# Gate/up stages of a two-sequence encoder layer: working buffers in neighbouring pairs, and 1024 columns per instruction where there were 512

## The chip, the cores and the metric

The kernel runs on one core of one Trainium2 chip. The metric is the device time of one execution in microseconds (us). Engines are named as the profile names them: PE is the matrix engine, PEld its weight load, DVE the vector engine, ACT the scalar engine, POOL the third general engine, and SPq the queue that issues nearly all DMA transfers. Each engine works through its own list of instructions in the order written for it, and an instruction that waits holds up everything behind it on that engine. A product sum is formed in a bank of PSUM, the memory that PE writes.

## The reference, cut to what matters

One encoder layer is applied to two sequences of 512 tokens, x_prompt and x_sample, with 1024 channels each, in float32. The layer is a half-weighted feed-forward part, a mixing part (attention beside an mLSTM memory, merged by gates), and a second half-weighted feed-forward part; a last norm follows. The feed-forward part is what the change touches:

```
def swiglu(x, w_gate, w_up, w_down):
    return (jax.nn.silu(x @ w_gate) * (x @ w_up)) @ w_down
x = x + 0.5 * swiglu(rms_norm(x, ffn1_norm), ffn1_w_gate, ffn1_w_up, ffn1_w_down)
...
x = x + 0.5 * swiglu(rms_norm(x, ffn2_norm), ffn2_w_gate, ffn2_w_up, ffn2_w_down)
```

w_gate and w_up are 1024 x 2816, w_down is 2816 x 1024. The width 2816 makes 22 blocks of 128 columns.

## The kernel before, in words

Float32 accuracy is got from a narrower matrix format (fp32r): a value is split into a part `hi`, made by a copy on ACT, and the remainder `lo = value - hi`, made by a subtraction on DVE. A product of two split matrices takes three matrix multiplications: hi with hi, hi with lo, lo with hi. So whatever goes into PE, weights and inputs, first costs one ACT and one DVE instruction of its size.

The gate and up products of a block, for both sequences together, form a two by two block product. The kernel does it with seven half-size products in place of eight (a scheme of Strassen's kind). For this it needs sums of weights and sums of inputs. The names are B11, B21, B22, T1, T2_, T3, T4, each a product of a weight half (4 slices of 128 rows) with an input tile `xc[...]` (512 columns wide, both hi and lo). One product is 4 slices times 3 matrix multiplications, that is 12 of 128 x 512.

A gate/up stage (there are two, one for each feed-forward part) runs thus:

- **Start.** `norm_x` and `turn` (stage one) or `turn_rows` (stage two) bring the inputs into place; `right_sums` forms the four sums of inputs per slice and `put` splits them into `xc`. While DVE and ACT do this, PE runs `begin(j)` for the first 7 blocks: products B11 and B21 only. Their two results, called v1 and g0, are parked in DRAM (`kept`). The first sequence's slices are parked in DRAM too (`xnbuf`) and loaded back for the sums.
- **Rest.** `rest` walks over the 22 blocks in the order `ORDER`: a block with kept results (5 products to do: T2_, T1, T3, B22, T4) alternates with a fresh block (7 products: B11, T2_, B21, T1, T3, B22, T4), seven times, and eight fresh blocks follow. Two blocks following each other make a pair here. The weights of the next block are made by `gu_left_a` (B11, B21), `gu_left_b` (T2_, T1, T3, B22) and `gu_left_c` (T4).
- **Out.** `gu_rest` adds the products up (bank Y takes T2_, T3, T4 one after the other, bank Z takes T1, B22) and forms gate times up: two results of 128 x 512 for a block. `Sides.even` and `Sides.odd` turn the four results of a pair into seven split matrices, the right sides of the down product, and write each hi and lo to DRAM (`rbuf`).

The stage that follows, `ffn_down`, reads `rbuf` and does the down product.

Buffers are rings. In `Rings`, `v` has 3 rows of 512 columns, `h` 5, `s` 3, `o` 7 and `wd` 2; rows are handed out one after the other, whatever becomes of the one before. Block number i (from 0) uses h rows 2i and 2i+1 (modulo 5) for g0 and the running sum u2 (lines 304, 305), and both rows stay in use as the in-place source of later sums and outputs: line 346 turns the even block's first result into the value of T1, line 338 writes its lo part over it, and the row is free once that DMA has landed.

Line 307 is the first reader of bank Y in a block: it forms u2 from v1 and the T2_ product, and only then may T3 be added in that bank. Between T2_ and T3 PE has the one product T1 to do in a block with kept results. A scheduler gives each engine its order: program order shifted by `SOONER` (sums that free a bank) or `LATER` (the `Sides` work), and then by its own model of when each instruction can run. Line numbers in the profile are those of the listing here.

In the mixing part the same pool of rows is used through `T2()`: 11 single rows under the tag "t2" and 4 under "f2", besides 2 rows "R" and a table tile whose first three rows serve the gate/up stages.

Of the kernel before, what the change touches and what calls it, by code (L numbers as in the profile page):

```python
# [16 lines left out]
P = 128  # L17
# [9 lines left out]
def encoder(ctx, tc, I, outs):  # L27
# [32 lines left out]
    def T2(dtype=F32, tag="t2"):  # L60
        if tag in ("eb", "ac"):
            i = boxes[tag]
            boxes[tag] += 1
            return boxes["tile"][:, i % 4 + (4 if tag == "ac" else 0), :]
        if tag == "R":
            return spool.tile([P, S], dtype, tag="R", bufs=2, name=nm("R"))
        n = {"t2": 11, "f2": 4}[tag]
        return tpool.tile([P, S], dtype, tag=tag, bufs=n, name=nm(tag))
# [14 lines left out]
    class Rings:  # L83


        def __init__(self, **kinds):
            self.rows = {k: [T2(F32, t) for t in tags] for k, tags in kinds.items()}
            self.at = dict.fromkeys(kinds, 0)

        def join(self, kind, *of):  # L90

            self.rows[kind] = [t for k in of for t in self.rows[k]]
            self.at[kind] = 0

        def rest(self, kind):

            rows = self.rows[kind]
            i = self.at[kind] % len(rows)
            return rows[i:] + rows[:i]

        def __call__(self, kind, dtype=F32):
            rows = self.rows[kind]
            t = rows[self.at[kind] % len(rows)]
            self.at[kind] += 1
            return t if dtype is F32 else t.bitcast(dtype)
# [124 lines left out]
    def right_sums(xc, k, x0l, x0u, x1l, x1u):  # L230
# [5 lines left out]
        for i, t in ((T1, x0l), (T2_, x1u), (T3, x1l), (T4, x0u)):  # L236
            put(xc[i], k, t)
# [17 lines left out]
    def gu_left_b(rg, ru, ring):  # L255
        v = lambda t: t.rearrange("p (k c) -> p k c", c=P)
        a, b = v(ring("s")), v(ring("s"))
        wb, wc = w8_tile(), w8_tile()
        V_.tensor_tensor(a, half(ru, 0), half(ru, 1), op=ALU.add)
        w_pair(wb[:, :, 1], a)  # L260
        V_.tensor_tensor(b, half(rg, 0), half(ru, 0), op=ALU.subtract)
        V_.tensor_tensor(a, a, half(rg, 0), op=ALU.subtract)  # L262
        w_pair(wb[:, :, 0], a)
        w_pair(wc[:, :, 0], b)
        V_.tensor_tensor(a, half(rg, 1), a, op=ALU.subtract)
        w_pair(wc[:, :, 1], a)
        return {T2_: part(wb, 0), T1: part(wb, 1), T3: part(wc, 0), B22: part(wc, 1)}

    def gu_left_c(ru, ring):
        wd = [ring("wd", F32R).rearrange("p (k c) -> p k c", c=P) for _ in range(2)]  # L270
        split(half(ru, 1), *wd)
        return {T4: wd}
# [23 lines left out]
    def gu_rest(W, xc, got, ring, mid):  # L296

        Y, Z = PS(), PT()
        second = lambda: product(Y, W[T2_], xc[T2_], True)
        if got:  # L300
            v1, g0 = got
            second()
        else:
            v1, g0 = gu_first(W, xc, lambda i: ring("vh"[i]), second)
        u2 = ring("h")
# [3 lines left out]
        v5 = ring("v")  # L309
# [16 lines left out]
        V_.tensor_tensor(g0, g0, v1, op=ALU.mult)  # L326
        V_.tensor_tensor(u2, u2, v5, op=ALU.mult)
        return g0, u2

    class Sides:  # L330


        def __init__(self, rb, ring):
            self.rb, self.ring = rb, ring

        def out(self, i, src, last=False):
            hi = self.ring("o")
            lo = src if last else self.ring("o")
            nc.scalar.activation(hi.bitcast(F32R), src, AF.Copy)
            V_.tensor_tensor(lo.bitcast(F32R), src, hi, op=ALU.subtract)  # L340
            nc.sync.dma_start(self.rb[i][:, 0, :], hi)
            nc.sync.dma_start(self.rb[i][:, 1, :], lo)

        def even(self, b11, b12):
            self.out(B11, b11)
            V_.tensor_tensor(b11, b12, b11, op=ALU.subtract)
            self.b = b11, b12

        def odd(self, b21, b22):
            t1, b12 = self.b  # L350
            self.out(B21, b21)
            self.out(B22, b22)
            V_.tensor_tensor(b12, b22, b12, op=ALU.subtract)
            self.out(T3, b12, True)
            V_.tensor_tensor(b22, b22, t1, op=ALU.subtract)
            self.out(T1, t1, True)
            V_.tensor_tensor(b21, b21, b22, op=ALU.subtract)
            self.out(T2_, b22, True)
            self.out(T4, b21, True)
# [6 lines left out]
    class Up:  # L366


        def __init__(self, xc, wg, wu, rb):
# [3 lines left out]
            self.ring = Rings(s=["t2"] * 3, wd=["f2"] * 2, v=["t2"] * 3, h=["t2"] * 5, o=["f2"] * 2 + ["R"] * 2)  # L373
            self.ring.rows["o"] += tables(FFN_ROWS)
            self.ring.join("x", "v", "h")
            self.ring.rows["k"], self.ring.at["k"] = self.ring.rows["o"][:2], 0
# [4 lines left out]
        def begin(self, j, W):  # L381

            self.kept[j] = kept[j]
            for t, d in zip(gu_first(W, self.xc, lambda _: self.ring("k")), kept[j]):
# [5 lines left out]
        def rest(self, raw, at=None, hook=None):  # L390
            ring = self.ring

            def resume(j):
                got = ring("v"), ring("h")
                for t, d in zip(got, self.kept.pop(j)):
                    nc.sync.dma_start(t, d)
                return got

            left = gu_left_b(*raw, ring)
            left.update(gu_left_c(raw[1], ring))  # L400
            raw = self.fetch(ORDER[1])
            got = resume(ORDER[0])
            for i, j in enumerate(ORDER):
                W = left
                nxt = ORDER[i + 1] if i + 1 < NF else None
                if nxt is not None:
                    left = {} if nxt in self.kept else gu_left_a(raw[0])
                    left.update(gu_left_b(*raw, ring))
                    ru = raw[1]
# [4 lines left out]
                if nxt is not None:  # L414
# [999 lines left out]
```

## Time and profile before

| what | value |
|---|---|
| median of 3 runs | 2124.43 us (2123.21 to 2124.66) |
| the profiled execution | 2124.45 us, its span 2122.7 us |
| busy | PE 98%, PEld 80%, DVE 74%, ACT 46%, POOL 5% |
| granted clock of PE, mean | 0.994 |
| gate/up stage one, first product to the down product | 20.42 to 458.14 us |
| gate/up stage two, the same | 1466.44 to 1898.43 us |
| DMA, mean over the span | 170 GB/s |

The profile counts time from the first instruction. A line of a group gives line number, engine, operation, output and input, size and count, then busy time, mean duration in ns, and idle time before with what ended it. The chain of waits follows the work back from the last instruction. The timeline lists instructions in order of time with start and duration, equal ones merged; a number in brackets is idle time before them and what ended it. Matrix multiplications overlap, so that a merged row's duration is somewhat longer than the distance from its start to the next.

### The profile page before, as it was taken

How to read it: one execution, taken by the hardware profiler on the slowest of the kernel's cores; microseconds unless marked ns; L12 is line 12 of the kernel's file. 1: busy time of each engine (PE TensorE's matmuls, PEld its weight loads, DVE VectorE, ACT ScalarE, POOL GpSimd, SP SyncE). 2: the span in 40 equal slices, each digit the busy share in tenths (PEclk: the TensorE clock that was granted, in tenths of full speed). 3: DMA queues.
4: the chain of work that ended last, by engine and by line, in shares of the span. 5: the costliest groups of instructions: out<-in, count | busy, mean ns of one | idle time of the engine just before them, and what ended most of it. 6: DMA issues, size and time to landing. Idle time of an engine off the chain costs nothing.

```text
span 2122.7 us, 26809 instructions
## 1 busy us (share of the span) xinstructions
PE 2070.4 (98%) x9472; PEld 1687.7 (80%) x9472; DVE 1581.2 (74%) x2817; ACT 968.5 (46%) x1739; POOL 107.2 (5%) x110
## 2 busy tenths in 40 slices
PE   6999999999999999999999999999999999999997
PEld 5887788888888777878887787788777888888885
DVE  7888787776796796574668855764988887786696
ACT  6544444442225466464435654544644444443223
POOL 0000000001000110100102001010000000000002
PEclk9999999999999999999999999999999999999998
DMA  8455554389764212232342122354454554479753
GB/s 272 150 195 194 182 188 144 133 300 395 270 230 158 74 66 68 92 114 88 120 158 80 60 90 74 135 171 157 164 194 163 199 172 159 144 262 389 287 205 121
DMA packets 141270, 361.81 MB, mean 170 GB/s; under 512 B 15600, under 2 KB 15616, under 8 KB 140112
## 3 DMA queue, kind: packets, MB, share of 16 engines
q1 hardware_dynamic: 140544, 358.84, 48.0%
q0 software_dynamic: 592, 1.27, 0.3%
q8 instruction: 74, 1.21, 0.2%
q14 instruction: 60, 0.49, 0.1%
HBM read 255.15 MB, written 104.89 MB: 170 GB/s over the span
## 4 chain that ended last, share of the span: by engine, by line
PE 81%; DVE 10%; ACT 4%; DMA 4%; issue 2%; POOL 0%; SPq 0%; ACTq 0%; DVEq 0%; POOLq 0%
PE pss L278 15%; PE mm L672 14%; PE pst L278 9%; PE mm L519 8%; PE mm L278 7%; PE pst L519 4%; PE pss L519 4%; PE mm L656 4%; PE mm L1099 3%; PE pso L519 3%; DMA rbuf<-t 2%; PE pso L926 2%; PE pso L656 1%; PE pso L1055 1%; PE pst L919 1%
## 5 line engine op out<-in xcount | busy, mean ns | idle before, releaser
L672 PE MATMUL mm<-xh,w 128*128 128x512 f32 x896 | 292.6, 396 | 0.0
L278 PE MATMUL pss<-xc,w 128*128 128x512 f32 x1056 | 258.1, 391 | 6.7 <-DVE t L307 6.5
L278 PE MATMUL mm<-xc,w 128*128 128x512 f32 x1056 | 256.2, 391 | 3.0 <-ACT f L287 2.6
L278 PE MATMUL pst<-xc,w 128*128 128x512 f32 x1056 | 255.4, 390 | 0.0
L278 PEld LDWEIGHTS pss<-xc,w 128*128 128x128 f32 x1056 | 196.5, 188 | 54.2 <-DVE t L307 13.6
L278 PEld LDWEIGHTS mm<-xc,w 128*128 128x128 f32 x1056 | 196.7, 188 | 47.7 <-ACT f L287 6.9
L278 PEld LDWEIGHTS pst<-xc,w 128*128 128x128 f32 x1056 | 197.3, 188 | 43.2 <-ACT t L311 2.5
L203 DVE TENSOR_TENSOR w<-wr,w 128x1024 fp32r<-128x1024 f32 (+1 forms) x112 | 135.9, 1215 | 105.5 <-ACT w L202 104.8
L672 PEld LDWEIGHTS mm<-xh,w 128*128 128x128 f32 x896 | 168.0, 189 | 32.2
L519 PE MATMUL mm<-w,rt 128*128 128x512 f32 x792 | 185.3, 389 | 0.0
L672 PE MATMUL mm<-xl,w 128*128 128x512 f32 x448 | 177.0, 395 | 0.0
L519 PEld LDWEIGHTS mm<-w,rt 128*128 128x128 f32 x792 | 148.4, 188 | 30.8
L240 ACT ACTIVATE w<-t 128x512 fp32r<-128x512 f32 x176 | 107.0, 628 | 121.3 <-DVE t L262 42.1
L202 ACT ACTIVATE w<-wr 128x1024 fp32r<-128x1024 f32 (+1 forms) x112 | 114.4, 1028 | 98.7 <-PE mm L672 29.3
L241 DVE TENSOR_TENSOR w<-t,w 128x512 fp32r<-128x512 f32 x176 | 118.1, 689 | 45.5 <-ACT w L240 42.4
L278 PE MATMUL pss<-xc,f 128*128 128x512 f32 x528 | 128.5, 392 | 0.0
L278 PEld LDWEIGHTS pss<-xc,f 128*128 128x128 f32 x528 | 98.2, 188 | 23.6 <-DVE t L315 3.6
L576 ACT ACTIVATE w<-wr 128x512 fp32r<-128x512 f32 x72 | 44.7, 631 | 132.2 <-PE pso L519 64.2
L576 ACT ACTIVATE w<-t 128x512 fp32r<-128x512 f32 x82 | 51.6, 632 | 116.0 <-PE pst L519 47.3
L672 PEld LDWEIGHTS mm<-xl,w 128*128 128x128 f32 x448 | 84.5, 189 | 15.7
L519 PE MATMUL pss<-w,rt 128*128 128x512 f32 x396 | 94.0, 389 | 0.0
L519 PE MATMUL pst<-w,rt 128*128 128x512 f32 x396 | 93.7, 389 | 0.0
(316 smaller groups left out, 3645.9 us busy)
## 6 DMA issues: line engine op xcount, KB each, us to landing
rt<-rbuf SPq DMA_DIRECT2D x154, 512.0 KB, 5.4
wr<-in_ffn_w_gate_dram SPq DMA_DIRECT2D x56, 512.0 KB, 4.3
wr<-in_w_in_cols_dram SPq DMA_DIRECT2D x56, 512.0 KB, 3.5
rbuf<-tab SPq DMA_DIRECT2D x90, 256.0 KB, 3.3
wr<-in_ffn_w_up_dram SPq DMA_DIRECT2D x44, 512.0 KB, 4.1
rbuf<-t SPq DMA_DIRECT2D x88, 256.0 KB, 3.3
rbuf<-f SPq DMA_DIRECT2D x66, 256.0 KB, 3.2
rbuf<-R SPq DMA_DIRECT2D x64, 256.0 KB, 3.1
```

Of the source, the lines that this page charges most:

```text
L202: pin(nc.scalar.activation(hi, raw, AF.Copy))
L203: pin(lo_eng.tensor_tensor(lo, raw, f(hi), op=ALU.subtract))
L240: pin(nc.scalar.activation(t[:, 0], src, AF.Copy))
L241: pin(V_.tensor_tensor(t[:, 1], src, f(t[:, 0]), op=ALU.subtract))
L278: nc.tensor.matmul(p, a[:, k, :], xt[:, b, k, :], start=(first and k == 0 and i == 0), stop=(k == HK_ - 1 and i == 2), skip_group_check=True)
L519: nc.tensor.matmul(p, r[:, b, d * P:(d + 1) * P], u[:, a, :], start=(first and q == 0 and k == 0), stop=(q == len(us) - 1 and k == 2), ski ...
L576: nc.scalar.activation(hi, src, AF.Copy)
L656: nc.tensor.matmul(p[b][:, :N], a[:, k, bs], w_[:, kl, :], start=(k == 0 and i == 0), stop=(k == KD - 1 and i == 2))
L672: nc.tensor.matmul(p, a[:, k, :], b, start=(k == 0 and i == 0), stop=(k == n - 1 and i == 2))
L919: nc.tensor.transpose(p[:, b * P:(b + 1) * P], Ps[b][:, kb * P:(kb + 1) * P], ident)
L926: nc.tensor.matmul(po, Vst[:, kv_, hk, :], w, start=(kv_ == 0 and i == 0), stop=(kv_ == 3 and i == 1))
L1099: nc.tensor.matmul(p[b], a[:, k, bs], w_[:, k - k0, :], start=(k == 0 and i == 0), stop=(k == KD - 1 and i == 2))
```

## The change

All working buffers of the stages become tiles of two neighbouring rows (1024 columns), and where two values lie side by side they are handled by one instruction:

- `Rings` with single rows is replaced by small `Ring`s: `v` has 2 pairs, `h` 3 pairs, `o` 3 pairs, `s` 2 single rows, `wd` 2 single rows. The pool has 6 pairs "t2", 2 pairs "f2" and one lone row; the 2 rows "R" are gone. A block takes one pair of `v` (v1, v5) and one of `h` (g0, u2).
- The weight sums T3 and T2_, B22 are formed in place in the fetched weights; T2_ with B22 and T3 with T4 are split as 1024 columns. T1's weights take the `wd` rows. T1, T3 and T4 are split in a second step, `more`, called after `gu_rest`.
- Gate times up is one multiplication of a pair.
- `Sides.out` splits and writes two right sides at once (T1 with T3, T4 with T2_, B21 with B22); B11 stays single. T4 and T2_ are formed in an extra pair `q`. `rbuf` becomes one DRAM tile for a pair of blocks, [128, 7, 2, 512].
- The inputs' sums work on two slices at once (`sums_of`); parking in `xnbuf` goes by pairs as well.
- In the mixing part `T2()` hands out halves of a pair, and `scores`, `attend` and `mem_out` take whole pairs.

The core of the diff:

```
-    def gu_left_b(rg, ru, ring):
...
-        V_.tensor_tensor(a, half(ru, 0), half(ru, 1), op=ALU.add)
-        w_pair(wb[:, :, 1], a)
-        V_.tensor_tensor(b, half(rg, 0), half(ru, 0), op=ALU.subtract)
-        V_.tensor_tensor(a, a, half(rg, 0), op=ALU.subtract)
-        w_pair(wb[:, :, 0], a)
-        w_pair(wc[:, :, 0], b)
-        V_.tensor_tensor(a, half(rg, 1), a, op=ALU.subtract)
-        w_pair(wc[:, :, 1], a)
...
-    def gu_left_c(ru, ring):
-        wd = [ring("wd", F32R).rearrange("p (k c) -> p k c", c=P) for _ in range(2)]
-        split(half(ru, 1), *wd)
+    def gu_left_b(rg, ru, ring, left):
+        (g0, g1_), (u0, u1) = [[half(r, i) for i in range(2)] for r in (rg, ru)]
+        a = v(ring.s())
+        V_.tensor_tensor(a, u0, u1, op=ALU.add)
+        V_.tensor_tensor(u0, g0, u0, op=ALU.subtract)
+        V_.tensor_tensor(g0, a, g0, op=ALU.subtract)
+        V_.tensor_tensor(g1_, g1_, g0, op=ALU.subtract)
+        wb = w8_tile()
+        w_pair(wb, halves(rg))
+        left.update({T2_: part(wb, 0), B22: part(wb, 1)})
+        def more():
+            wd = [v(ring.wd(F32R)) for _ in range(2)]
+            split(a, *wd)
+            wc = w8_tile()
+            w_pair(wc, halves(ru))
+            left.update({T1: wd, T3: part(wc, 0), T4: part(wc, 1)})
+        return more
...
+        v, h = got or (ring.v(), ring.h())
+        v1, v5 = v[:, 0], v[:, 1]
+        g0, u2 = h[:, 0], h[:, 1]
...
-        V_.tensor_tensor(g0, g0, v1, op=ALU.mult)
-        V_.tensor_tensor(u2, u2, v5, op=ALU.mult)
-        return g0, u2
+        V_.tensor_tensor(h, h, v, op=ALU.mult)
+        return h
...
+        def out(self, ms, src):
+            hi, lo = self.o(), src
+            if ms.stop - ms.start == 1:
+                hi, lo = hi[:, 0:1], hi[:, 1:2]
             nc.scalar.activation(hi.bitcast(F32R), src, AF.Copy)
             V_.tensor_tensor(lo.bitcast(F32R), src, hi, op=ALU.subtract)
+            nc.sync.dma_start(self.rb[:, ms, 0, :], hi)
+            nc.sync.dma_start(self.rb[:, ms, 1, :], lo)
...
+        def odd(self, b2):
+            b1, q = self.b1, self.o()
+            b21, b22 = b2[:, 0], b2[:, 1]
+            V_.tensor_tensor(b1[:, 1], b22, b1[:, 1], op=ALU.subtract)
+            V_.tensor_tensor(q[:, 1], b22, b1[:, 0], op=ALU.subtract)
+            V_.tensor_tensor(q[:, 0], b21, q[:, 1], op=ALU.subtract)
+            self.out(slice(T1, T3 + 1, T3 - T1), b1)
+            self.out(slice(T4, T2_ + 1, T2_ - T4), q)
+            self.out(slice(B21, B22 + 1), b2)
...
-            self.ring = Rings(s=["t2"] * 3, wd=["f2"] * 2, v=["t2"] * 3, h=["t2"] * 5, o=["f2"] * 2 + ["R"] * 2)
+            r.v, r.h = Ring(wide("t2") for _ in range(2)), Ring(wide("t2") for _ in range(3))
+            r.s = Ring([lone, tab[:, 2 * S:3 * S]])
+            r.wd = Ring([fa[:, i] for i in range(2)])
+            r.o = Ring([fb, tab[:, 0:2 * S].rearrange("p (a c) -> p a c", c=S), wide("t2")])
+            r.x = Ring(r.v.rows + r.h.rows)
...
+    def sums_of(k, turned, gain):
+        x0l, x0u, x1l, x1u = [up.ring.x() for _ in range(4)]
+        nc.sync.dma_start(x0l, xnbuf[:, k:k + 2, :])
+        nc.sync.dma_start(x0u, xnbuf[:, k + HK_:k + HK_ + 2, :])
+        for c in range(2):
+            for t, kk, bank in ((x1l, k + c, PS), (x1u, k + c + HK_, PT)):
+                nc.scalar.activation(t[:, c], turned(kk, bank), AF.Copy, scale=gain[:, kk:kk + 1])
+        put(xc[B22], slice(k, k + 2), x1u)
+        right_sums(xc, k, x0l, x0u, x1l, x1u)
...
-                e = T2()
+                if b % 2 == 0:
+                    both = pair()
+                e = both[b % 2]
...
-                    ph, pl = T2(F32R), T2(F32R)
+                    ph, pl = pair(dtype=F32R)
```

More of the change, by code (lines that the diff above doesn't have):

```diff
@@ L81, in tables, with __init__, rest, __call__ @@
         return out
[L83 to L104, printed above, removed]
+    class Ring:
+        def __init__(self, rows):
+            self.rows, self.at = list(rows), 0
+        def rest(self):
+            i = self.at % len(self.rows)
+            return self.rows[i:] + self.rows[:i]
+        def __call__(self, dtype=F32):
+            t = self.rows[self.at % len(self.rows)]
+            self.at += 1
             return t if dtype is F32 else t.bitcast(dtype)
@@ L383, in begin @@
             self.kept[j] = kept[j]
-            for t, d in zip(gu_first(W, self.xc, lambda _: self.ring("k")), kept[j]):
+            for t, d in zip(gu_first(W, self.xc, lambda _: self.ring.k()), kept[j]):
                 nc.sync.dma_start(d, t)
@@ L1308, in encoder @@
         xc[i] = xc_tile()
[L1309 to L1314 removed]
+    for k in (0, 2):
         W.append(up.left(3 + k))
[L1316 to L1317 removed]
+        sums_of(k, lambda kk, bank: turn_rows(rows1, kk, bank), g2)
+        W.append(up.left(4 + k))
     for j in (3, 4, 5, 6):
```

143 lines of the change are left out of this document (61 added, 82 removed).

## The prediction

> **What bounds the kernel now.** The head of the page comes first: the span, and what each engine was busy in it.
>
> ```profile
> span 2122.7 us, 26809 instructions
> PE 2070.4 (98%) x9472; PEld 1687.7 (80%) x9472; DVE 1581.2 (74%) x2817; ACT 968.5 (46%) x1739; POOL 107.2 (5%) x110
> ```
>
> PE is busy 98% of the span, so an edit that shortens DVE or ACT work pays only where PE stands still for it. Outside PE's busy time there are 2122.7 - 2070.4 = 52.3 us in the whole kernel. What of them lies in the gate/up stages is read from PE's timeline (start, duration, line, count, idle time before).
>
> ```profile
> 20.42 2.56 PE L278 MATMUL mm<-xc,w 128*128 128x512 f32 x10
> 68.22 3.06 PE L278 MATMUL mm<-xc,w 128*128 128x512 f32 x12 [0.27 <-ACT f L287]
> 441.82 2.88 PE L278 MATMUL pss<-xc,w 128*128 128x512 f32 x12
> 444.54 2.88 PE L278 MATMUL mm<-xc,w 128*128 128x512 f32 x12
> 458.14 6.28 PE L519 MATMUL mm<-w,rt 128*128 128x512 f32 x27
> 1466.44 9.61 PE L278 MATMUL mm<-xc,w 128*128 128x512 f32 x41
> 1508.08 3.06 PE L278 MATMUL mm<-xc,w 128*128 128x512 f32 x12 [0.28 <-ACT f L287]
> 1898.43 6.28 PE L519 MATMUL mm<-w,rt 128*128 128x512 f32 x27
> ```
>
> Two products that follow without a gap start 444.54 - 441.82 = 2.72 us apart, 0.2267 us per multiplication. A stage needs 22 x 7 x 12 = 1848 of them; 161 of them begin before 68.22 in stage one and 158 before 1508.08 in stage two. So the rest of stage one, 458.14 - 68.22 = 389.9 us for 1687 (382.4 us), loses 7.5 us; the rest of stage two, 390.4 us for 1690 (383.1 us), loses 7.3 us. The starts lose about 7 and 2 us (47.8 us against 36.5 for products and about 4 for transposes; 41.6 against 35.8 and 3.5). Nothing the change does in the rests can give more than 7.5 + 7.3 = 14.8 us.
>
> Where the rests lose it, the chain of waits and the timeline show. These are the starts of the fresh blocks' first product, and one place between:
>
> ```profile
> 122.39 2.72 PE mm L278 x12
> 155.39 2.72 PE mm L278 x12
> 177.44 0.61 DVE t L340
> 178.07 3.98 DMA rbuf<-t
> 182.07 0.70 DVE t L307
> 189.87 2.72 PE mm L278 x12
> 225.03 2.72 PE mm L278 x12
> 258.31 2.72 PE mm L278 x12
> ```
>
> ```profile
> 182.81 3.94 PE L278 MATMUL pss<-xc,w 128*128 128x512 f32 x16 [1.27 <-DVE t L307]
> 217.99 3.92 PE L278 MATMUL pss<-xc,w 128*128 128x512 f32 x16 [1.95 <-DVE t L307]
> ```
>
> A pair of a kept and a fresh block is 12 products, 12 x 2.72 = 32.6 us. The distances are 33.0, 34.5, 35.2, 33.3 us. The long ones hold a stop at L307: DVE makes lo of an earlier block's side (L340, 177.44), SP sends it, it lands 4 us later at 182.05, and only then may L307 write u2 into that row. T3 waits for L307 because it adds into the same bank; the only cover is product T1, 2.72 us. How often, by the view of that line (us, times):
>
> ```profile
> its engine sat idle before it (us, times) until:
>   DMA rbuf<-t: 11.4, 13
> who waited for it (us, times):
>   PEld pss L278: 13.6, 20
>   PE pss L278: 6.5, 8
> ```
>
> PE stood 6.5 us in 8 places. A pair with a stop is longer by more than the stop itself: 34.5 - 33.0 = 1.5 for 1.27, 35.2 - 33.0 = 2.2 for 1.95, so 0.2 more each. Together 6.5 + 8 x 0.2 = 8.1 us, the largest single loss in the rests. (PEld's 13.6 run beside PE's own work; only the 6.5 stopped PE.)
>
> **The change part by part.**
>
> *The ring h.* Before, 5 rows at two rows per block: u2 of a block takes the row that g0 of two blocks earlier left, the one whose lo goes out last. After, three pairs: a block takes what the block three earlier left, a whole block (five products 13.6 us, seven 19.0 us) more time. In the changed order DVE makes the lo of T1 and T3 some 8 us into a kept block; with landing that is before 14 us, and the first taker, the next block's g0, comes at 19. The lo of B21 and B22 comes some 18 us in, lands by 23, and its taker, u2 of the kept block after that, comes at 35. So L307's wait for `rbuf` goes: -8.1 us. What is late next: in a kept block u2 is now reached by DVE later, behind the work of `Sides` and the sums; its T2_ product ends at 32.6 + 2.72 = 35.3 us from the start of the pair before, DVE reaches u2 at about 35.7 and ends it at 36.4 (an estimate from the order and the starts below), and T3 is due at 38.1, so 1.7 us of cover are left. If that is gone, each us more stops PE for a us.
>
> *Wide instructions.* DVE's times from start to start, where it was not waiting:
>
> ```profile
> 187.16 0.68 DVE L317 TENSOR_TENSOR t<-t,t 128x512 f32<-128x512 f32 x1
> 187.76 0.69 DVE L262 TENSOR_TENSOR t<-t,wr 128x512 f32<-128x512 f32 x1
> 197.72 1.22 DVE L241 TENSOR_TENSOR w<-wr,w 128x1024 fp32r<-128x1024 f32 x1
> 198.86 0.68 DVE L315 TENSOR_TENSOR t<-t,pss 128x512 f32<-128x512 f32 x1
> ```
>
> 512 columns take 0.60 us, 1024 take 1.14. A pair of blocks has 43 narrow and 1 wide instruction on DVE before (27.1 us), 25 narrow and 10 wide after (26.4 us): 0.7 us less in a pair of at least 32.6 us. Over 22 pairs that is 15 us of DVE, none on PE's path, since DVE has more time than work there:
>
> ```profile
> 190.00:260.00 70.00, 67.95 (x297) 54.89 (x296) 57.82 (x92) 29.03 (x49) 0.00 (x0) 1.00 0.53 184
> ```
>
> (A stretch of the mixed blocks: length, then busy time of PE, PEld, DVE, ACT, POOL, then clock, DMA share, GB/s.) DVE is busy 57.8 of 70 us. The worth on the path is 0; bounds: 0 and the 0.7 us at each pair where DVE is last. The Trainium skill ("VectorE: DVE Perf Modes", section "The DRAIN you can't avoid") has an operation start only when the pipe is empty, with (N + 151)/0.96 ns, which is 691 and 1224 ns, and advises to minimize the number of operations. By it two narrow ones merged would save 157 ns, where the starts above give 70; the durations agree with it (0.68, 1.22), the distances don't, and the measurement decides. By that rule DVE would save 1.4 us a pair, and the end would not move, as PE stays last.
>
> *Weights.* T1, T3 and T4 are split in `more`, behind `gu_rest`. The splits are needed from 5.4 us of the next block on, and PE's waits in the changed order stay the same kinds. DVE works in order, so L259 (L263 after), which waits for the fetched up weights, holds up the sums that free banks:
>
> ```profile
> DVE t L259 <- DMA wr<-in_ffn_w_up_dram: 12.4, 15, 1.4
> ```
>
> 15 times, 1.4 us at most. After, about 1.9 us are tolerated at that place. I take 0; bounds -1 and +4.
>
> *Writes.* 14 transfers of 256 KB a pair become 2 of 256 and 6 of 512 KB, the same bytes. SP spends 0.32 us on each:
>
> ```profile
> L341 SPq DMA_DIRECT2D rbuf<-tab x29: 319/320/680, 103.9 to 424.9; - x29
> ```
>
> so 6 x 0.32 = 1.9 us less SP per pair, hidden, as SP waits most of the time. A transfer takes longer to land, which matters where a row is waited for. Times from issue to landing:
>
> ```profile
> wr<-in_ffn_w_gate_dram SPq DMA_DIRECT2D x56, 512.0 KB, 4.3
> rt<-rbuf SPq DMA_DIRECT2D x154, 512.0 KB, 5.4
> DMA to landing us min/median/max: 2.0/3.2/9.6
> ```
>
> The last row is that of the 256 KB writes to `rbuf` in stage one. I take 4.3 us, the row of the same size in the same stage; 3.2 and 5.4 are the ends, 9.6 the worst seen. The Trainium skill ("DMA: Bandwidth & Descriptors", section "Anatomy of one DMA — SWDGE (gpsimd) path") puts a transfer at 2 us plus bytes over 436 GB/s, an estimate of 3.2 us for 512 KB; the rows are above it, and nothing here rests on it.
>
> *The ring o.* With three pairs and five takers per pair of blocks, the hi of B21/B22 takes the row in which q was, and must wait until the lo of T4/T2_ has landed. ACT waits there, and behind it stands its copy of v1 (L292), which PE needs for product B21 at 7 x 2.72 = 19.0 us of the pair. DVE gets to that lo after T2_ (2.72), six narrow and three wide instructions: 2.72 + 6 x 0.60 + 3 x 1.14 = 9.8, with about 0.5 for hand-overs 10.3. Then 0.4 for issue, L for landing, 1.06 for the wide copy and twice 0.6 for the narrow ones:
>
> ```profile
> L240 ACT ACTIVATE w<-wr 128x1024 fp32r<-128x1024 f32 x44 | 46.6, 1060 | 45.4 <-PE pst L278 30.1 <-PE pso L1099 8.8 <-PE pss L278 3.3
> L240 ACT ACTIVATE w<-t 128x512 fp32r<-128x512 f32 x176 | 107.0, 628 | 121.3 <-DVE t L262 42.1 <-PE pst L278 38.7 <-DVE t L265 20.8
> ```
>
> Slack: 19.0 - (10.3 + 0.4 + L + 1.06 + 1.23) = 6.0 - L. With L = 4.3 there are 1.7 us left; transfers as late as 9.6 are seldom, and I add 0.8 us over both stages for this and for the u2 place (two stops of 0.4). Bounds: 0, and rival B.
>
> *Starts.* Sums on two slices at once: nine wide instructions for every 18 narrow ones, over a stage 20.5 instead of 21.8 us of DVE, a gain of at most 1.3 us. Against it: a slice pair needs 4 of 5 pairs of the ring x, so the next one must wait for the last `put`, a wait of up to 3 us. DVE was nearly full there (39.2 of 42 us):
>
> ```profile
> 30.00:72.00 42.00, 38.27 (x177) 29.87 (x176) 39.17 (x74) 31.45 (x52) 0.00 (x0) 1.00 0.72 238
> ```
>
> I take 0 per stage; bounds -1.3 and +3.
>
> *Mixing part.* 11 single rows become 12 halves of 6 pairs, f2 4 rows become 2 pairs, R goes; a half is free only with its pair. PE waits there now at few places:
>
> ```profile
> 719.82 1.07 PE L842 MATMUL pst<-ident,t 128*128 128x128 f32 x8 [2.14 <-DVE t L577]
> 1133.69 0.73 PE L900 MATMUL pss<-kv,qT 128*128 128x512 f32 x2 [2.19 <-ACT t L905]
> ```
>
> One row more, but coarser. I take 0; bounds -4.3 and +4.3 (these two stops gone, or as much again). The down products keep their buffers and read the same bytes: 0.
>
> **Sum.** The profiled run took 2124.45 us (span 2122.7 and 1.7 around it), which is the median of the runs, 2124.43. 2124.45 - 8.1 + 0.8 + 0 (starts, mix, weights, writes) = 2117.1, so **2117 us**.
>
> **The rivals.**
>
> A, *no change that can be told*: L307's stops go, but both starts lose their 3 us at the ring x, so 2117 + 2 x 3 = 2123 us. For it: DVE has no reserve there. Against it: the sums of the first sequence come from DRAM and need little of DVE before they are split.
>
> B, *slower*: ACT stands before the hi of B21/B22 until q's lo has landed, and v1 is late for B21. It decides at L > 6.0 us, and from there every us is a us of PE. At L = 7 in the 14 kept blocks of both stages that is 14 x 1.0 = 14 us, so 2131 us. For it: writes have taken up to 9.6 us, and every transfer after is twice as large. Against it: the median of that size is 4.3, and the load in the stage is 153 to 240 GB/s before and no more after. By the page's estimate of 3.2 us the Trainium skill would leave 2.8 us of slack, against B as well.
>
> C, *more*: with L307 go also the remaining hand-overs of the rests, all 14.8 us with nothing new: 2124.45 - 14.8 = 2109.7, so 2110 us.
>
> **How the numbers follow.** About 0.2% (4.2 us, below 2120.2 or above 2128.7) is what a measurement of this kernel can tell from no change. Forecast 0.58 (its own range 2112 to 2120.2), A 0.20, B 0.16, C 0.06. Faster: 0.58 + 0.06 = 0.64; same 0.20; slower 0.16. The range of 8 in 10 goes from C's 2109 to just before B's middle, 2130.
>
> **What would show it.** Right: at u2 (L313) no idle time for `rbuf`, the pairs of mixed blocks at 33.0 to 33.4 us; DVE's wide subtraction at 1.14 us from start to start, DVE busy about 20 us less by durations, PE's idle time 7 us less. The starts within 1.5 us of 47.8 and 41.6 us. Wrong: PE idle before product B21 after ACT L292, with ACT waiting for `rbuf` at L345 (B); PE idle in the start for ACT or DVE behind x (A); PE idle at T3 for L313 because DVE comes late, not a transfer; new stops in the mix beside those two rows.

## The result, and the profile after

The changed kernel takes 2118.65 us in the median of 12 runs (2114.99 to 2122.63); the kernel before, run beside it, 2123.96 us (2121.95 to 2128.45). The ratio is 0.9972, with an interval of 0.9963 to 0.9981: 4 to 8 us faster. The profiled execution took 2116.60 us, 2 us below its median, so the differences between the two traces, which sum to 7.8 us, are somewhat larger than that of the medians, 5.3.

The head of the changed kernel's page:

```profile
span 2114.8 us, 26230 instructions
PE 2068.3 (98%) x9472; PEld 1692.4 (80%) x9472; DVE 1558.7 (74%) x2583; ACT 940.2 (44%) x1565; POOL 103.2 (5%) x110
```

DVE is busy 22.5 us less (1581.2 before) in 234 fewer instructions; PE has the same 9472. PE's timeline of the changed kernel, at the ends of the two gate/up stages, near the ends of their starts (68.28, 1507.24) and at two fresh blocks (start, duration, line, count):

```profile
20.33 2.55 PE L283 MATMUL mm<-xc,w 128*128 128x512 f32 x10
...
68.28 1.07 PE L283 MATMUL pss<-xc,w 128*128 128x512 f32 x4
...
148.18 2.88 PE L283 MATMUL mm<-xc,w 128*128 128x512 f32 x12
...
180.82 2.88 PE L283 MATMUL mm<-xc,w 128*128 128x512 f32 x12
...
450.10 6.28 PE L533 MATMUL mm<-w,rt 128*128 128x512 f32 x27
...
1464.52 10.06 PE L283 MATMUL mm<-xc,w 128*128 128x512 f32 x43
...
1507.24 3.02 PE L283 MATMUL mm<-xc,w 128*128 128x512 f32 x12
...
1889.57 6.28 PE L533 MATMUL mm<-w,rt 128*128 128x512 f32 x27
```

Set against the rows of before, this gives where the time went:

| stretch | before, us | after, us | difference |
|---|---|---|---|
| stage one, first product to down product | 437.72 | 429.77 | -7.95 |
| middle (down products, mixing part) | 1008.30 | 1014.42 | +6.12 |
| stage two | 431.99 | 425.05 | -6.94 |
| from its down products to the end of the span | 224.27 | 225.23 | +0.96 |

The stages gave 14.9 us, twice what was forecast, and the middle took 6.1 back. (The last 0.96 us were not followed up.) A pair of blocks now takes 180.82 - 148.18 = 32.64 us, which is 12 products of 2.72 without a gap. L313, the line that forms u2 (L307 before), waits for no write any more (what its engine waited for, and who waited for it):

```profile
L313 DVE TENSOR_TENSOR t<-t,pss x44: 675/679/687, 73.6 to 1877.5; 128x512 f32<-128x512 f32 x44
...
its engine sat idle before it (us, times) until:
  PE pss L283: 0.6, 1
who waited for it (us, times):
  PEld pss L283: 0.2, 1
```

The loss in the middle lies in the two runs of attention heads, one for each sequence. They begin with the transposes of the rotated queries (L842 before, L856 after) and end where the memory part's reciprocals are turned (L185, L187). Before, the further marks beside the 719.82 already shown:

```profile
916.76 0.62 PE L185 MATMUL pst<-ident,rs 128*128 128x128 f32 x4 [0.47 <-DVE rs L168]
1122.47 1.06 PE L842 MATMUL pst<-ident,t 128*128 128x128 f32 x8 [1.49 <-DVE t L577]
1313.55 0.62 PE L185 MATMUL pst<-ident,rs 128*128 128x128 f32 x4 [0.47 <-DVE rs L168]
```

After:

```profile
711.96 1.06 PE L856 MATMUL pst<-ident,t 128*128 128x128 f32 x8 [0.57 <-DVE t L591]
911.14 0.62 PE L187 MATMUL pst<-ident,rs 128*128 128x128 f32 x4 [0.47 <-DVE rs L170]
1115.90 1.06 PE L856 MATMUL pst<-ident,t 128*128 128x128 f32 x8 [0.47 <-DVE t L591]
1312.07 0.62 PE L187 MATMUL pst<-ident,rs 128*128 128x128 f32 x4 [0.45 <-DVE rs L170]
```

The first run of heads went from 196.94 to 199.18 us, the second from 191.08 to 196.17, together +7.3, with no stop in the marks themselves that would account for it; other stretches of the middle are 1.2 us shorter in sum.

### The profile page after: what moved, and what is told of

It is laid out like the page before. It is cut to its first block, busy times and chain, and to the rows that moved or that the text cites. A ratio compares the mean times of both kernels' runs of the same rounds, so it can differ in the third digit from the quotient of the medians.

```text
span 2114.8 us, 26230 instructions
## 1 busy us (share of the span) xinstructions
PE 2068.3 (98%) x9472; PEld 1692.4 (80%) x9472; DVE 1558.7 (74%) x2583; ACT 940.2 (44%) x1565; POOL 103.2 (5%) x110
## 4 chain that ended last, share of the span: by engine, by line
PE 86%; DVE 7%; ACT 3%; DMA 2%; issue 1%; SPq 0%; POOL 0%; DVEq 0%; ACTq 0%; POOLq 0%
PE pss L283 17%; PE mm L686 14%; PE pst L283 11%; PE mm L283 10%; PE mm L533 7%; PE mm L670 4%; PE pst L533 4%; PE pss L533 4%; PE mm L1115 3%; PE pso L533 2%; PE pso L942 2%; PE pso L670 1%; PE pso L1071 1%; PE pss L914 1%; PE pss L1022 1%; PE pso L1115 1%
## 5 line engine op out<-in xcount | busy, mean ns | idle before, releaser
L283 PE MATMUL pss<-xc,w 128*128 128x512 f32 x1584 | 379.1, 389 | 0.0
L283 PEld LDWEIGHTS pss<-xc,w 128*128 128x128 f32 x1584 | 297.2, 188 | 62.0 <-DVE t L313 0.2
L242 ACT ACTIVATE w<-wr 128x1024 fp32r<-128x1024 f32 x132 | 139.7, 1060 | 235.3 <-PE pst L283 142.0
L243 DVE TENSOR_TENSOR w<-wr,w 128x1024 fp32r<-128x1024 f32 x132 | 161.1, 1222 | 80.2 <-ACT w L242 79.9
L283 PE MATMUL pst<-xc,w 128*128 128x512 f32 x528 | 127.1, 389 | 0.0
L283 PE MATMUL pst<-xc,f 128*128 128x512 f32 x528 | 127.0, 389 | 0.0
L283 PEld LDWEIGHTS pst<-xc,w 128*128 128x128 f32 x528 | 99.0, 188 | 20.8 <-ACT t L316 0.3
L283 PEld LDWEIGHTS pst<-xc,f 128*128 128x128 f32 x528 | 99.1, 188 | 20.6
L590 ACT ACTIVATE w<-t 128x512 fp32r<-128x512 f32 x82 | 51.6, 632 | 121.8 <-PE pst L533 63.6
L590 ACT ACTIVATE w<-wr 128x512 fp32r<-128x512 f32 x72 | 44.6, 631 | 129.8 <-PE pso L533 65.7
```

The source lines that it names most:

```text
L242: pin(nc.scalar.activation(t[:, 0], src, AF.Copy))
L243: pin(V_.tensor_tensor(t[:, 1], src, f(t[:, 0]), op=ALU.subtract))
L283: nc.tensor.matmul(p, a[:, k, :], xt[:, b, k, :], start=(first and k == 0 and i == 0), stop=(k == HK_ - 1 and i == 2), skip_group_check=True)
L590: nc.scalar.activation(hi, src, AF.Copy)
```

## The experiments

All times below are medians of 5 rounds unless said otherwise, with the ratio to runs of the kernel before on the same chip. The stretches are read from PE's timeline of one profile each, as in the table above. They vary from one execution to the next: the runs of one kernel spread over 2 to 8 us, and the profiled run of an experiment lies up to 4.4 us from its median. So a middle is taken as known to some 2 to 4 us; no kernel was profiled twice.

| kernel | stage one | middle | stage two | time, us | ratio, interval |
|---|---|---|---|---|---|
| third h pair, else as before | 430.77 | 1007.24 | 425.76 | 2110.28 | 0.9931, 0.9918 to 0.9945 |
| changed kernel, narrow | 430.14 | 1013.87 | 425.31 | 2116.82 | 0.9963, 0.9950 to 0.9975 |
| before, pool in pairs | 436.68 | 1016.16 | 435.40 | 2130.73 | 1.0024, 1.0013 to 1.0034 |
| third h pair, f2 in pairs | 430.36 | 1007.23 | 424.79 | 2108.56 | 0.9922, 0.9908 to 0.9935 |
| third h pair, t2 in pairs | 429.69 | 1012.88 | 424.15 | 2115.12 | 0.9954, 0.9942 to 0.9967 |
| third h pair, both in pairs | 429.78 | 1016.10 | 424.52 | 2115.78 | 0.9953, 0.9940 to 0.9965 |
| 9 t2 rows, 4 rows p1 | 428.63 | 1017.55 | 424.56 | 2115.49 | 0.9953, 0.9940 to 0.9965 |
| 9 t2 rows, 2 pairs p1 | 428.49 | 1013.54 | 424.57 | 2110.70 | 0.9929, 0.9915 to 0.9943 |
| changed kernel, q's lo late (3 rounds) | 429.59 | 1021.51 | 425.47 | 2136.18 | 1.0051, 1.0035 to 1.0068 |
| 13 t2 rows | 430.60 | 1009.28 | 425.23 | 2110.69 | 0.9935, 0.9923 to 0.9948 |
| 10 t2 rows | 428.91 | 1009.52 | 425.08 | 2111.28 | 0.9937, 0.9924 to 0.9951 |
| 7 t2 pairs, 3 f2 rows | 429.51 | 1008.69 | 424.35 | 2110.31 | 0.9931, 0.9918 to 0.9943 |

**Only the third pair in the ring h.** One row more in h, taken from the ring s of the weight sums:

```
-            self.ring = Rings(s=["t2"] * 3, ..., h=["t2"] * 5, ...)
+            self.ring = Rings(s=["t2"] * 2, ..., h=["t2"] * 6, ...)
             self.ring.join("x", "v", "h")
+            self.ring.rows["x"].pop()
...
-        (va, *v2), (ha, *h4) = ring.rest("v"), ring.rest("h")
+        (va, *v2), (ha, hb, *h4) = ring.rest("v"), ring.rest("h")
-        s1s = ring.rows["s"]
+        s1s = ring.rows["s"] + [hb]
```

> The kernel before with one row more in the ring h (6 instead of 5, the row taken from the ring s), all else narrow and single as before. Theory R (the ring): every stop of the rests hangs on L307's wait for rbuf, the short ones too that the idle column of the matrix engine doesn't show; then the rests of both stages, 389.9 and 390.4 us, go down to 383 to 384.5, the middle between the stages stays at 1008 (+-1.5), and the time is 2124 - 12 = 2112 us (2110 to 2114.5). Theory W (the ring gives the 8 us of the forecast, and the wide instructions the other 7): rests at 386 us each, 2116 us. Theory D (DVE's amount of work sets the rests): L307 late for another reason, 2121 us or more.

It came out as theory R says, 2110.28 us, faster than both kernels. The stages lost 6.95 and 6.23 us of their time, 13.2 together, and the middle stayed. PE's timeline of this kernel at the stages' ends:

```profile
21.16 1.18 PE L278 MATMUL mm<-xc,w 128*128 128x512 f32 x4
...
451.93 1.30 PE L520 MATMUL mm<-w,rt 128*128 128x512 f32 x5
...
1459.17 1.07 PE L278 MATMUL mm<-xc,w 128*128 128x512 f32 x4
...
1884.93 1.30 PE L520 MATMUL mm<-w,rt 128*128 128x512 f32 x5
```

and what L307's engine waited for, and who waited for it:

```profile
its engine sat idle before it (us, times) until:
  PE pss L278: 3.4, 4
  DMA rbuf<-R: 2.7, 2
  DMA rbuf<-f: 2.7, 2
  DMA rbuf<-tab: 1.4, 1
who waited for it (us, times):
```

There are waits for `rbuf` left, 6.8 us in 5, but the list of those who waited for L307 is empty. One row of 256 KB is enough for nearly all that the changed kernel gains in its stages (14.9 us). The 1.7 us that are missing are no more than the kernels with this ring differ by among themselves (the table).

**The changed kernel with narrow instructions.**

```
-        w_pair(wb, halves(rg))
+        for i in range(2):
+            w_pair(wb[:, :, i], half(rg, i))
...
-            w_pair(wc, halves(ru))
+            for i in range(2):
+                w_pair(wc[:, :, i], half(ru, i))
...
-        V_.tensor_tensor(h, h, v, op=ALU.mult)
+        for i in range(2):
+            V_.tensor_tensor(h[:, i], h[:, i], v[:, i], op=ALU.mult)
...
-            nc.scalar.activation(hi.bitcast(F32R), src, AF.Copy)
-            V_.tensor_tensor(lo.bitcast(F32R), src, hi, op=ALU.subtract)
+            for i in range(1 if ms.stop - ms.start == 1 else 2):
+                nc.scalar.activation(hi[:, i].bitcast(F32R), src[:, i], AF.Copy)
+                V_.tensor_tensor(lo[:, i].bitcast(F32R), src[:, i], hi[:, i], op=ALU.subtract)
```

> The changed kernel with its rings and transfers, but narrow instructions again in the rests: the splits of T2_ with B22 and of T3 with T4, gate times up, and the hi and lo of the pairs of right sides are each two instructions of 512 columns. Theory R: the rests don't need the wide instructions, each stage stays within 1.5 us of the changed kernel's 429.8 and 425.1 us, and the time within 2 us of its 2118.7. Theory W: some 0.7 us per pair of blocks come back where DVE is last, 5 to 15 us: 2124 to 2133 us.

Theory R again. The head of its page:

```profile
span 2114.9 us, 26505 instructions
PE 2069.8 (98%) x9472; PEld 1695.3 (80%) x9472; DVE 1568.4 (74%) x2781; ACT 955.7 (45%) x1719; POOL 104.0 (5%) x110
```

DVE has 198 instructions more than in the changed kernel and ACT 154, and the stages are within 0.4 us of it, the span within 0.1. The wide instructions in the rests are worth nothing on this path. The Trainium skill ("VectorE: DVE Perf Modes", section "Rules for kernel authors") advises to minimize the number of operations. Here fewer of them meant less busy time of DVE (1558.7 against 1568.4 us) and no less time of the kernel.

**Only the pool and the mixing part.** The stages are those of the kernel before; the pool's code is the changed kernel's (`wide`, `pair` and `T2` as in the diff), and

```
-            self.ring = Rings(s=["t2"] * 3, wd=["f2"] * 2, v=["t2"] * 3, h=["t2"] * 5, o=["f2"] * 2 + ["R"] * 2)
+            self.ring = Rings(wd=["f2"] * 2, v=["t2"] * 3, h=["t2"] * 5, s=["t2"] * 3, o=["f2"] * 2 + ["t2"])
+            self.ring.rows["o"].append(lone)
...
-                e = T2()
+                if b % 2 == 0:
+                    both = pair()
+                e = both[b % 2]
...
-                    ph, pl = T2(F32R), T2(F32R)
+                    ph, pl = pair(dtype=F32R)
```

> The stages as in the kernel before (five single rows in h, narrow), the pool and the mixing part as in the changed kernel (halves of six pairs and of two pairs, whole pairs in scores, attend and mem_out). Theory M (the coarser pool costs the middle its time): between the stages 1014 us instead of 1008, 2130 us. Theory O (the 6 us lie in the order that the planner came to in the changed kernel, not in the pool): the middle at 1007 to 1010 us, 2124 us. In both the rests lose their 7 us each at L307 as before.

Theory M: 2130.73 us, slower than the kernel before, and its interval excludes 1; the middle is 1016.2. So the pool in pairs costs some 5 to 8 us by itself, in a kernel whose stages are the old ones (the ratio gives 5.1, the profile's middle 7.9). The profiled run took 2134.45 us, 3.7 more than the median, and its stage two is 3.4 us longer than before; why was not followed up. The stages keep their stops:

```profile
PE pss L288 <- DVE t L317: 8.2, 9, 1.7
```

(From this kernel's list of PE's waits: L317 is its line for u2; us in total, times, longest.)

**Which tag.** Three kernels, all with the third h pair and narrow stages. The first turns only f2 into pairs, the second only t2, the third both:

```
-        n = {"t2": 11, "f2": 4}[tag]
-        return tpool.tile([P, S], dtype, tag=tag, bufs=n, name=nm(tag))
+        if not odd_half[tag]:
+            odd_half[tag].extend(reversed(pair(tag)))
+        t = odd_half[tag].pop()
+        return t if dtype is F32 else t.bitcast(dtype)
```

(in the first two, the tag that stays single keeps the old line; t2 in pairs brings `pair()` into `scores`, `attend` and `mem_out`).

> The kernel with the third h pair (six rows, single and narrow; 2110 us, its middle 1007.2 us), and only the tag f2 handed out as halves of two pairs in place of four rows; t2 stays eleven single rows. Theory F (the two rows in which attend's sums are formed are held until their pair is free): the middle between the stages goes to 1013 to 1016, 2117 us. Theory T (the t2 pairs of the probabilities cost it): the middle stays at 1006 to 1009, 2110 us.

> The same kernel, with only the tag t2 handed out as halves of six pairs, whole pairs in scores, attend and mem_out; f2 stays four single rows. Theory T: the middle 1013 to 1016, 2117 us. Theory F: 1006 to 1009, 2110 us. If neither does it alone, both this and the run with f2 in pairs stay below 1010.

> The same kernel with both tags in pairs, that is, narrow stages with the third h pair and the changed kernel's mixing part. If the ring h and the pool in pairs are all that counts of the change: stages 430 and 425.5 us, middle 1014 to 1016, 2118 us, as the changed kernel's 2118.7 within 2 us. If the wide instructions or the wide transfers are worth something after all: 2121 us or more.

f2 in pairs costs nothing, and is with 2108.56 us the fastest median of all, though its interval overlaps that of the single rows. t2 in pairs costs 5.6 us in the middle and 4.8 in the median. With both, 2115.78 us: this kernel has the changed kernel's ring and pool and none of its wide instructions or wide transfers, and it is not slower than the changed kernel. A ring that reaches one block further and a pool of coarser grain are thus all of the change that shows in the time.

**What in the t2 pairs.** One place shows it. The view of attend's product (the line that multiplies the values with the split, turned probabilities) lists who waited for it. In the changed kernel:

```profile
who waited for it (us, times):
  ACT t L590: 22.6, 14
  ACT f L950: 13.2, 9
```

and in the same list of the kernel before:

```profile
  ACT f L934: 4.1, 8
```

ACT's next hi (L590, into a t2 row) now waits for PE to be done with an earlier pair, and PE then waits for that hi: by the distances between starts in PE's timeline less 0.2267 us for each multiplication (0.11 for each transpose), it loses some 6 us ahead of that product in the changed kernel and none before. By the same count the product of `mem_out`, which reads pairs of the same kind, loses 2 us more than before (4.6 against 2.6). Two readings were possible: the pair is freed only as a whole (grain), or there are too few rows at hand (room). Two kernels gave attend and mem_out four rows of their own, once as single rows, once as two pairs:

```
-        if tag == "R":
-            return spool.tile([P, S], dtype, tag="R", bufs=2, name=nm("R"))
-        n = {"t2": 11, "f2": 4}[tag]
+        n = {"t2": 9, "f2": 4, "p1": 4}[tag]
...
-                    ph, pl = T2(F32R), T2(F32R)
+                    ph, pl = T2(F32R, "p1"), T2(F32R, "p1")
```

> The kernel with the third h pair (six rows), with the split probabilities of attend and the split values of mem_out in four single rows of their own (tag p1, taken from R and from two of the eleven t2 rows). Theory G (the grain: a pair comes free only with the later of the two products that read it, and ACT's next hi waits for that): with single rows the middle stays at 1006 to 1009 us, and the matrix engine loses under 1.5 us ahead of attend's product; 2109 us. Theory N (it is a matter of how many rows there are and who shares them): 1011 us or more, as t2 has two rows less.

> The same, but the four rows p1 are two pairs; the number of rows and who shares them is the same. Theory G: the middle 1012 to 1016 us, ACT waits for attend's product some 20 us in the whole, the matrix engine loses 4 to 6 us ahead of that product; 2115 us. Theory N: within 1.5 us of the run with single rows.

Theory G falls. With single rows the time is 2115.49 us, with pairs 2110.70: the wrong way round. Theory N had the first number right (a middle of 1017.55, where it said 1011 or more) and the second wrong: the two kernels lie 4 us apart in the middle and 4.8 in the time, where it allowed 1.5. In both, ACT no longer waits for attend's product with its hi, and the loss has moved to the scores, which have nine rows left of t2 (PE's waits, first for single rows, then for pairs):

```profile
PE pss L899 <- ACT t L904: 6.7, 5, 2.8
```

```profile
PE pss L907 <- ACT t L912: 6.0, 4, 2.4
```

(3.2 us in 3 in the kernel with the third h pair.) So the number of rows was varied by itself.

```
-        n = {"t2": 11, "f2": 4}[tag]
+        n = {"t2": 13, "f2": 4}[tag]
```

```
-        return tpool.tile([P, 2, S], F32, tag=tag, bufs={"t2": 6}[tag], name=nm(tag))
+        return tpool.tile([P, 2, S], F32, tag=tag, bufs={"t2": 7}[tag], name=nm(tag))
```

(the rows come from R and, for the seventh pair, from f2 and the lone row; the run with ten moves one to R).

> The kernel with the third h pair (six rows, eleven single t2 rows, middle 1007.2 us, 2110 us) with thirteen single t2 rows in place of eleven, the two of R added to them. Theory S (room: the mixing part needs rows free for the scores of the next head, so its time falls as rows are added): the middle at 1007 us or less, 2110 us or less. Theory Q (chance of the order: every change of the pool gives the planner another order of the mixing part, and eleven single rows happen to have a good one): the middle anywhere from 1006 to 1017 us, without regard to the number.

> The same with ten single t2 rows (the eleventh moved to R, which the mixing part doesn't use). Theory S: the middle 1009 to 1014 us, between the 1007 of eleven and the 1017.6 of nine with four of their own, 2112 to 2117 us. Theory Q: anywhere from 1006 to 1017 us.

> The kernel with t2 in pairs (six pairs, middle 1012.9 us) with seven pairs, the row taken from f2 (three single rows in place of four) and the lone row. Theory S: the middle falls to 1009 us or less, 2111 us. Theory Q: it stays at 1012 or more, or goes either way without order. (If three rows of f2 are too few, the matrix engine waits for ACT's f copies in the heads, and the run tells nothing of t2.)

Ten, eleven and thirteen single rows give a middle of 1007 to 1009.5 us, without order, and the same time; thirteen miss theory S's 1007. Six pairs, twelve rows, give 1012.9, and seven pairs 1008.7 and 2110.31 us. The lists of those who waited for attend's product say more than the middles do. With six pairs and the third h pair, ACT's hi waits as in the changed kernel:

```profile
  ACT t L593: 23.0, 14
```

With seven pairs this wait is gone, and only ACT's f copies are in the list:

```profile
  ACT f L951: 16.6, 12
```

(They don't lengthen the middle, 1008.7 us.) With eleven and thirteen single rows nothing there waits for a t2 row. With ten, DVE's lo begins to be:

```profile
  DVE t L578: 3.7, 4
```

Ahead of that product PE loses about 5.5 us with six pairs, 2.4 with ten single rows, and 0.6 or less with seven pairs, eleven or thirteen rows. So six pairs serve the heads worse than ten single rows, and a seventh pair mends it: it is room, and the grain takes room away. Theory S stands in that form; its smaller steps don't show in the time, and differences of 2 us in the middle follow no order, as theory Q would have them. No run held the order fixed: the kernels with six pairs have nearly the same order of ACT's work in the heads, those with single rows another, and the one with seven pairs is nearer to the former; how much of the cost lies in the order itself is open. Which long-lived half keeps its pair occupied was not traced.

**Rival B: a late write.** Four extra writes of q's lo to a scratch tile, ahead of its own:

```
+            if ms == slice(T4, T2_ + 1, T2_ - T4):
+                for i in range(4):
+                    nc.sync.dma_start(extra[:, i], lo)
             nc.sync.dma_start(self.rb[:, ms, 1, :], lo)
```

> The changed kernel with four more writes of q's lo (512 KB each, to a scratch tile) ahead of its own, so that q's row comes free later; they are extra work. Rival B's mechanism, tried on purpose: in the trace of the changed kernel the slack of ACT's copy of v1 is about 2 us. If the landing moves from 5 to some 9 us, PE stands some 2 us ahead of product B21 in each of the 14 kept blocks, with ACT in front of L345 waiting for rbuf: 28 us, 2146 us. If ACT had more room than the forecast says, 2119 to 2124 us.

Neither expectation held: the time is 2136.18 us, but with both stages as quick as in the changed kernel. ACT's timeline shows why. In the changed kernel (the bracket is idle time and what ended it):

```profile
183.19 1.07 ACT L345 ACTIVATE t<-t 128x1024 fp32r<-128x1024 f32 x1 [1.11 <-DMA rbuf<-t]
...
184.68 0.58 ACT L292 ACTIVATE t<-mm 128x512 f32<-128x512 f32 x1
```

With the late lo:

```profile
184.19 0.58 ACT L292 ACTIVATE t<-mm 128x512 f32<-128x512 f32 x1
...
190.68 1.05 ACT L345 ACTIVATE t<-t 128x1024 fp32r<-128x1024 f32 x1
```

The scheduler, it seems, plans with the extra writes: the hi of B21/B22 (L345) now stands behind the copy of v1 (L292). The run therefore doesn't price the rival. What it cost, 7 us in the middle and 8 at the end, lies elsewhere, 11.7 us of it in the down products' wait for their right sides:

```profile
PE pss L536 <- DMA rt<-rbuf: 11.7, 3, 6.0
```

A write that is slow on the chip but not in the scheduler's model was not tried.

## Why the prediction was right, and where two of its terms were not

The time, 2118.65 us, lies 1.6 us from the 2117 forecast and within the narrow range; faster was right, and so was the wait that had to go. That the number came out is luck: two errors cancel, 7.6 us too little gain in the stages and 6.1 us too little loss in the middle.

*The ring h: the mechanism right, the size half.* Forecast -8.1, measured -13.2 by the ring alone and -14.9 in the changed kernel. The step that failed is "(PEld's 13.6 run beside PE's own work; only the 6.5 stopped PE.)". In the pairs that the prediction took as free of stops (33.0 and 33.3 us) L307 was late as well, only by less. PE and PEld at one such place before:

```profile
249.43 5.76 PE L278 MATMUL pss<-xc,w 128*128 128x512 f32 x23
...
250.53 0.69 DVE L307 TENSOR_TENSOR t<-t,pss 128x512 f32<-128x512 f32 x1 [0.56 <-DMA rbuf<-t]
251.27 3.50 PEld L278 LDWEIGHTS pss<-xc,w 128*128 128x128 f32 x16 [0.52 <-DVE t L307]
...
255.06 3.01 PE L278 MATMUL pss<-xc,f 128*128 128x512 f32 x12
```

DVE waits 0.56 us for the write, PEld 0.52 us for DVE, and PE's row carries no idle time at all: a matmul's recorded duration (0.39 us in the page's groups) is longer than its distance to the next (0.2267), so a small stop vanishes in the overlap, or leaves too little to be listed. Only the distance between starts shows it: the 23 multiplications from 249.43 to 255.06 take 5.63 us where 23 x 0.2267 is 5.21. By these distances, over both rests, PE lost some 10.6 us at the products that wait for L307, not 8.1; another 1.8 stood at the products after them, whose weight load waits for L315, and 0.9 elsewhere. With the third h pair alone 0.7 us are left of it all, so those small hand-overs went with L307's. The 13.6 us of PEld, 20 times, were the better estimate. Rival C had the right size, 14.8, for the stages; it was given 6 in 100 because the other 6.7 us were taken for hand-overs that would stay. The forecast of 33.0 to 33.4 us for a pair of mixed blocks has the same error: it kept the small stops, and the pairs take 32.64.

*The middle: taken as 0, measured +6.1, beyond the +4.3 given as its bound.* The step that failed is "One row more, but coarser. I take 0". The bound was taken from the stops that were there; the cost came from new ones, ahead of attend's product, most too short for PE's idle column. Rows before could not show it, and no rival had it, though "new stops in the mix" stood among the signs of being wrong.

*New waits at u2: +0.8 forecast, none found.* PE has no stop in either rest.

*Rival B was near.* The changed kernel's trace at the tightest place of stage two:

```profile
1559.29 0.58 ACT L292 ACTIVATE t<-mm 128x512 f32<-128x512 f32 x1
...
1560.45 0.84 PE L283 MATMUL mm<-xc,w 128*128 128x512 f32 x3
```

The copy of v1 ends 0.58 us before product B21 begins; in a fresh block where ACT doesn't wait for the write it is 1.92. So it is in 9 of the 14 pairs with kept blocks; in the other five 0.58 to 1.61 are left (1.0 at the place shown above, 184.68 + 0.58 to 186.26). So the rival never became due. The forecast left 1.7 us in every pair; the landing it took, 4.3 us, lies between two cases. In the median it was too long:

```profile
rbuf<-t SPq DMA_DIRECT2D x72, 512.0 KB, 3.2
rbuf<-tab SPq DMA_DIRECT2D x30, 512.0 KB, 3.6
```

The wide writes land after 3.2 to 3.6 us in the median by these rows, hardly later than the narrow ones did (3.1 to 3.3). Where ACT waited it was too short: at the place shown above SP issued the write at 177.86, and ACT went on at 183.19; it landed after 5.25 us, and the prediction's 6.0 - L gives 0.75 for that, near the 1.0 measured. The 9.6 us that the prediction has as the worst write, and that rival B leans on, belong to a read: the view of `rbuf` takes in the first reads `rt<-rbuf` of the down product. In a window that ends before these, the longest write of stage one took 6.0 us before, and 5.4 after. The median is near the estimate from the Trainium skill's page ("DMA: Bandwidth & Descriptors", section "Anatomy of one DMA — SWDGE (gpsimd) path"), 3.2 us, which the prediction set below the rows of reads. The page's fit is of transfers issued by GpSimd, and SP issues these; and the same rule gives 2.6 us for 256 KB, where the rows have 3.1 to 3.3. So the agreement at 512 KB may be chance.

*Starts: 0 forecast, and so it is.* From 68.28 to 450.10 us PE runs without a gap, 381.82 / 0.2267 = 1684 multiplications, as many as are left of the 1848. The other 164 (37.2 us) and about 4 us of transposes stand in the 47.95 us before, which lose 7 us, as before the change; by the same count (163 of them before 1507.24) stage two's start loses 2.3 us against 2. Rival A's wait at the ring x did not come.

*Wide instructions: 0 forecast, 0 measured.* DVE's distances in the changed kernel:

```profile
198.78 1.22 DVE L243 TENSOR_TENSOR w<-wr,w 128x1024 fp32r<-128x1024 f32 x1
199.92 0.68 DVE L266 TENSOR_TENSOR wr<-wr 128x512 f32<-128x512 f32 x1
```

The wide one takes 1.14 us from start to start, as before, and DVE is busy 22.5 us less where 20 were expected. The prediction's own rows give a little less by distances than it took from them: 2 x 0.60 - 1.14 is 60 ns, not 70, and a pair of blocks 26.9 us before, not 27.1, so 0.5 us less a pair and not 0.7. The term was 0 either way. The section of the Trainium skill that the prediction sets against these distances ("VectorE: DVE Perf Modes", "The DRAIN you can't avoid") also says that a next operation that is not held starts earlier; the starts here agree, 0.08 us before the recorded end of the one in front (0.68 against 0.60, 1.22 against 1.14).

*Weights: 0.* DVE's wait for the up weights fell in stage one from 12.4 us in 15 to

```profile
DVE t L263 <- DMA wr<-in_ffn_w_up_dram: 0.8, 3, 0.3
```

## What to carry to other kernels

Read the loss of a dense stretch of PE from the distances between starts, not from the idle column: here stops of up to 0.37 us left no listed idle time, and the idle column showed 6.5 of the 13.2 us that the ring cost; the weight load's waits name their cause. Read also what a view takes in: the worst landing of a tile may be that of its reads. Before a rewrite for a ring that comes round too early, try one more row in it: that row was worth more (2110.3 us) than the whole change (2118.7). Merging neighbouring buffers for wider instructions makes the pool coarser for every other user of it, and twelve rows in six pairs served the mixing part here worse than ten single ones.

## What the runs showed of the hardware that was not expected

A 512 KB write to `rbuf` landed after 3.2 to 3.6 us in the median, the 256 KB writes before after 3.1 to 3.3, so that doubling the size of these transfers cost at most half a microsecond; the longest in stage one took 5.4 us, and 6.0 before. Writes issued while the down products read their right sides took up to 14.7 us before and 16.1 after. The dense products can run without any stop over a whole rest: 381.8 us at 0.2267 us for each multiplication, with the writes of the right sides and the weight loads beside them.
